# The mLSTM's two key groups as one pair of seven products, woven with a query group and the value groups

## The chip, the cores and the metric

The kernel runs on one core of one Trainium2 chip. The time is the device time of one execution in microseconds; of the kernel before, three runs gave 2150.21 to 2151.62 us, with a median of 2151.44 us.

## The reference

One layer of an encoder trunk over 256 rows of 2048 channels, in float32. Two SwiGLU feed-forward blocks stand around a mixer, each followed by a layer norm. The mixer multiplies the first norm's output by one wide matrix and cuts the product into columns:

```python
x = _layer_norm(ALPHA * x + 0.5 * _swiglu(x, ffn1_w1[i], ffn1_w3[i], ffn1_w2[i]), ln1_g[i], ln1_b[i])
mix = _hybrid_mixer(x, w_in[i], b_gates_m[i], conv_m[i], norm_m[i], w_up_m[i], w_up_sb[i], w_out[i])
...
proj = x @ w_in
mq, mk, mv, mo, mi, mf, sq, sk, sv, ga, gb = _split_cols(proj)
qk = jax.nn.silu(_causal_conv(jnp.concatenate([mq, mk], axis=-1), conv_w))
q_m, k_m = jnp.split(qk, 2, axis=-1)
```

`mq` and `mk` are the mLSTM's queries and keys (1024 columns each, four heads of 256), `mv` its values, `mo` its output gates, `mi` and `mf` its input and forget gates (four columns each); `sq`, `sk` and `sv` belong to the stick-breaking attention, `ga` and `gb` gate the two branches' sum. Queries and keys go through a short causal convolution along the rows and a SiLU.

## The kernel before, in words

**Units, splits, queues.** TensorE multiplies in pieces: each weight block of 256 rows by 512 columns (`raw`, 128 partitions x 1024 values) and each activation tile is held as a high and a low half (`split`, `actT`), and three matmuls, high by high, high by low and low by high, make one product (L1468 to L1470). A *unit* is one block against one half (128) of the rows: two steps of 128 weight rows with three matmuls each, six of 128x512. A block comes in by a DMA on the SP queue (`loads`, L1370), ScalarE writes its high half (L1393), VectorE the low half (L1397), and only then can the unit's second matmul start. Six split blocks are held at a time in the mixer, and raw blocks up to a limit that depends on the stage (`HELD`: 6 in the stage "mix", 10 in "woven", 12 in "wide"). Raw blocks, splits, activation tiles and larger intermediate results (`big`) share 51 pages of SBUF.

**Plain groups and pairs.** A plain group (`group`) is 512 columns of a weight over all 2048 rows: 8 blocks, each used by two units, one for each half of the rows, so 16 units. A pair (`seven`, `both7`) takes two such groups together by a scheme of seven products in place of eight for each quarter of the weight's rows: 28 units, each with a block of its own. Some of these blocks are sums of raw blocks. Each sum is either an addition on VectorE (L444) or, for the quarters listed in `loaded`, a DMA on GpSimd's queue that adds onto the raw block (L450). `every` lists all quarters, with two sums by VectorE in each; `later` leaves out the first, whose four sums are all VectorE's. A pair also needs a second kind of activation tiles, its *forms*, sums and differences of the halves of the transposed rows (`form_turn`, L382 to L386, then split by L358 and L359). The results of the seven products are put together by `both7`'s `done` and `rest` on ScalarE and VectorE.

**Order.** The program is a list of units, with small generators beside it that fall due at written delays (`sched.spawn`). Pairs stand in a `side` list that `weave` distributes among the plain units of a `main` list in proportion. Each engine works through its own instructions in the order in which the program made them.

**Around the change.** The first norm transposes its rows in pieces (`Norm.turn`, L363), applies gain and bias to the transposed values (L295) and splits them into the tiles of `x1T`. With `ActT(..., True)` the transposed values lie in a temporary tile that is dropped, and `forms_later` (L394 to L401) later adds the high and low halves again (L399) and makes the forms. The norm's rows themselves are scaled by VectorE (`affine`, L622), their bias is added by a DMA on GpSimd's queue (L626), and each then leaves for DRAM on the SP queue (`put_away`, L331). After the first feed-forward block come the first query group (16 units), the group with the gates and two stick-breaking heads (16 units of 264 columns), the second query group and the two key groups, all plain. Then two value groups, the stick-breaking columns and the branch gates follow as `main`, woven with five pairs as `side`. A query or key group is copied to two temporary tiles by `qk_done`, and `conv` transposes it, runs the convolution on VectorE (L890) and the SiLU on ScalarE. `gates` (L827 to L855) and the generators `mlstm`, `stick` and `gated` run beside the units, each as soon as its inputs are flagged.

Of the kernel before, what the change touches and what calls it, by code (L numbers as in the profile page):

```python
# [11 lines left out]
ALU = mybir.AluOpType  # L12
# [225 lines left out]
def kernel(  # L238
# [39 lines left out]
    def big(shape=(P, 1024)):  # L278
        return page_pool.tile(list(shape), F32, name="big", tag="page")
# [113 lines left out]

    def forms_later(act, c):  # L394

        act.whole[c] = big()
        for t in range(TT):
            hi, lo = (act.tiles[c, t][:, k].rearrange("q k s -> q (k s)") for k in range(2))
            nc.vector.tensor_tensor(out=act.whole[c][:, t * COL:(t + 1) * COL], in0=hi, in1=lo, op=ALU.add)  # L399
        yield 4.0  # L400
        yield from form_turn(act, c)  # L401


    def rows_of(w, r, col0, cols):
# [350 lines left out]

    x1T = ActT(act_tile, ActT(act_tile), True)
    norm1 = Norm(ln1_g[0], ln1_b[0], gb1, x1T, (24.0, 3.0), put_away)
# [101 lines left out]
    def qk_done(which, g):  # L859
        stage = {}  # L860

        def done(ps, t):
            stage[t] = temp()
            nc.scalar.copy(stage[t][:], ps)
            if t == TT - 1:
                sched.spawn(conv(which, g, stage), DELAY["cv0"])
        return done

    def conv(which, g, stage):
        for e in range(2):  # L870
# [25 lines left out]
            yield DELAY["cv2"]  # L896
        drop(2)

# [207 lines left out]
    program.extend(flat(group(w_in, range(0, D, 2 * P), 4096, 2 * HM + 2 * DS, x1T, gates_done)))  # L1106
    for which, g in ((0, 1), (1, 0), (1, 1)):
        program.extend(flat(group(w_in, range(0, D, 2 * P), which * 1024 + g * COL, COL, x1T, qk_done(which, g))))
        if which == 0:
            program.append(lambda: [sched.spawn(forms_later(x1T, c), 4.0 + 12.0 * c) for c in range(4)])  # L1110
    program.append(lambda: [sched.spawn(in_sequence([mlstm(a), mlstm(a + 1)])) for a in (0, 2)])

    def v(g):
# [70 lines left out]
    def pair(g):  # L1184
# [4 lines left out]
    gate = branch(0, 1)  # L1189
    main = v(0) + v(1) + sb(*SB_GROUPS[0]) + sb(*SB_GROUPS[1]) + [Mode("wide")] + sb(*SB_GROUPS[2]) + sb(*SB_GROUPS[3]) + [lambda: sched.spawn(lane())] + branch(0, 0) + gate[:4] + bring_ym_back(gate[4:] + ups(0)) + ups(1) + ups(2)  # L1190
    mode("woven")
    program.extend(weave(main, in_line([both7(w_in, sq0 + 2 * HS * DS, sq0 + 2 * HS * DS + COL, x1T, sv_dest, sv_ready, later),
                                   both7(w_in, 3072, 3072 + COL, x1T, mo_dest, mo_ready, every), pair(1), pair(2), pair(3)])))
    mode("mix")
# [164 lines left out]
    def pieces(j):  # L1359
        return [slice(0, 1), slice(1, 2)] if j < 2 else [slice(0, 2)]  # L1360

    def loads(most=len(raws)):
        while pos["load"] < most and pos["raw"] < (4 if pos["at"] < 6 else limits(pos["split"])[0]):
            j = pos["load"]
            r = raws[j]
            r.tile = page_pool.tile([P, 2, COL], F32, name="raw", tag="page")
            dst, src = r.tile[:, :, :r.cols], r.src
            if r.cols == COL:
                dst, src = whole(dst), whole(src)
            nc.sync.dma_start(out=dst, in_=src)  # L1370
            pos["load"] += 1
            pos["raw"] += 1

    def make(j):
# [9 lines left out]
    def split_one():  # L1384
# [15 lines left out]
        pos["split"] += 1  # L1400
        for f in w.soon:
            assert f.raw.tile is not None
            f.make()
            f.made = True
        pos["raw"] -= len(w.frees)
# [120 lines left out]
```

## Time and profile before

| | |
|---|---|
| median of three runs | 2151.44 us |
| the profiled execution | 2150.85 us |
| its span, first to last instruction | 2149.1 us |
| share of TensorE, weight loads, VectorE, ScalarE, GpSimd | 100%, 83%, 87%, 70%, 7% |
| granted TensorE clock | 1.00 |
| DMA traffic | 537 MB, 250 GB/s in the mean |

The span is cut into instructions with start, duration and the instruction or transfer that ended the wait before them. Engines are named PE (TensorE), PEld (its weight loads), DVE (VectorE), ACT (ScalarE), POOL (GpSimd) and SP (the queue of most DMAs). Records of neighbouring matmuls overlap, as do those of neighbouring VectorE instructions, so what one costs in a row is read from start to start. L numbers are lines of the kernel before, unless a row of the new order is shown. The mixer begins near 688 us.

### The profile page before, as it was taken

The numbers are of one execution on the slowest core, as the hardware profiler recorded it, in microseconds if no ns is written. First come the engines' busy times: TensorE is split into PE (matmuls) and PEld (weight loads), VectorE is DVE, ScalarE is ACT, GpSimd is POOL, SyncE is SP. The second block draws the span as 40 slices with busy tenths as digits, with TensorE's granted clock in tenths as the row PEclk, the third lists the DMA queues.
The fourth block names the chain that finished last, engine by engine and source line by source line (L and its number), as shares of the span: only waits on it lengthen the run. The fifth ranks groups of instructions, "written<-read, shape, count | busy, mean of one in ns | idle before, by whom it ended". The sixth has DMA issues, their size and how long they took to land. (4 is left out here: it accounts for less than half of the span.)

```text
span 2149.1 us, 27832 instructions
## 1 busy us (share of the span) xinstructions
PE 2140.6 (100%) x9742; PEld 1774.0 (83%) x9742; DVE 1864.1 (87%) x2002; ACT 1499.8 (70%) x1947; POOL 161.1 (7%) x190
## 2 busy tenths in 40 slices
PE   9999999999999999999999999999999999999998
PEld 7888888888888888888888888888888888888887
DVE  7899989899987798878888999799998998989763
ACT  6676777767767665778876667757676776776872
POOL 0011000011000000000000000011000011000000
PEclk9999999999999999999999999999999999999999
DMA  9799788988894776868898888789878898889562
GB/s 363 232 265 268 245 264 245 280 266 272 263 310 156 213 262 200 257 205 217 261 282 264 269 235 293 236 226 264 263 246 249 275 279 263 262 260 282 216 180 109
DMA packets 151963, 537.02 MB, mean 250 GB/s; under 512 B 17168, under 2 KB 21776, under 8 KB 151824
## 3 DMA queue, kind: packets, MB, share of 16 engines
q1 hardware_dynamic: 125616, 439.82, 57.2%
q0 software_dynamic: 26208, 95.43, 23.7%
q8 instruction: 76, 1.25, 0.2%
q14 instruction: 63, 0.52, 0.1%
HBM read 528.90 MB, written 6.29 MB: 249 GB/s over the span
## 5 line engine op out<-in xcount | busy, mean ns | idle before, releaser
L1397 DVE TENSOR_TENSOR split<-raw,split 128x1024 fp32r<-128x1024 f32 (+1 forms) x1102 | 1294.8, 1210 | 157.5 <-ACT split L1393 148.7
L1393 ACT CAST split<-raw 128x1024 fp32r<-128x1024 f32 (+1 forms) x1102 | 1106.9, 1043 | 353.6 <-DVE raw L444 118.4
L1468 PE MATMUL mm<-split,actT 128*128 128x512 f32 x3056 | 1196.8, 392 | 0.5 <-ACT actT L358 0.4
L1470 PE MATMUL mm<-split,actT 128*128 128x512 f32 x3056 | 1183.9, 387 | 0.0
L1469 PE MATMUL mm<-split,actT 128*128 128x512 f32 x3056 | 1182.9, 387 | 0.6 <-DVE split L1397 0.4
L1470 PEld LDWEIGHTS mm<-split,actT 128*128 128x128 f32 x3056 | 573.7, 188 | 118.8 <-DVE actT L359 0.4
L1469 PEld LDWEIGHTS mm<-split,actT 128*128 128x128 f32 x3056 | 574.4, 188 | 114.9 <-DVE split L1397 2.1
L1468 PEld LDWEIGHTS mm<-split,actT 128*128 128x128 f32 x3056 | 574.1, 188 | 114.8 <-issue 1.0
L444 DVE TENSOR_TENSOR raw<-raw 128x1024 f32<-128x1024 f32 x214 | 260.7, 1220 | 2.3
L450 POOL DMA_DIRECT2D raw<-in_ffn_w_dram x124 | 109.0, 998 | 1028.5 <-DVE split L1397 883.2
L359 DVE TENSOR_TENSOR actT<-temp,actT 128x512 fp32r<-128x512 f32 (+1 forms) x94 | 62.6, 682 | 49.3 <-ACT actT L358 49.3
L295 ACT ACTIVATE temp<-mm 128x512 f32<-128x512 f32 (+1 forms) x54 | 31.2, 583 | 76.4 <-PE mm L1470 76.2
L718 ACT COPY big<-mm 128x512 f32<-128x512 f32 x80 | 46.8, 585 | 28.9 <-PE mm L1470 28.5
L358 ACT CAST actT<-temp 128x512 fp32r<-128x512 f32 (+1 forms) x94 | 56.9, 616 | 13.0 <-DVE temp L383 7.1
L450 POOL DMA_DIRECT2D raw<-in_w_in_dram x38 | 33.3, 990 | 407.5 <-DVE split L1397 394.9
L371 ACT COPY temp<-ms 128x512 f32<-128x512 f32 x44 | 25.9, 588 | 44.4 <-PE ms L363 43.8
L725 ACT COPY mm<-big 128x512 f32<-128x512 f32 x96 | 55.8, 589 | 0.0
L662 DVE TENSOR_TENSOR temp<-mm,temp 128x512 f32<-128x512 f32 x72 | 49.6, 688 | 5.0 <-PE mm L1470 3.8
L626 POOL DMA_DIRECT2D big<-in_ln_b_dram x12 | 10.4, 865 | 351.7 <-DVE big L622 218.2
L1313 DVE TENSOR_TENSOR temp<-temp,big 128x512 f32<-128x512 f32 (+1 forms) x10 | 5.8, 584 | 32.5 <-ACT temp L295 32.5
L291 ACT ACT_TABLE_LOAD x26 | 33.4, 1283 | 0.5
L359 DVE TENSOR_TENSOR actT<-big,actT 128x512 fp32r<-128x512 f32 x24 | 16.4, 689 | 11.6 <-ACT actT L358 11.6
(140 smaller groups left out, 636.1 us busy)
## 6 DMA issues: line engine op xcount, KB each, us to landing
raw<-in_ffn_w_dram SPq DMA_DIRECT2D x528, 512.0 KB, 6.2
raw<-in_w_in_dram SPq DMA_DIRECT2D x168, 512.0 KB, 5.6
raw<-in_ffn_w_dram POOLq DMA_DIRECT2D x124, 512.0 KB, 8.8
raw<-in_w_in_dram POOLq DMA_DIRECT2D x38, 512.0 KB, 8.3
raw<-in_w_out_dram SPq DMA_DIRECT2D x32, 512.0 KB, 4.7
raw<-in_w_ple_gate_dram SPq DMA_DIRECT2D x32, 512.0 KB, 4.5
raw<-in_w_up_m_dram SPq DMA_DIRECT2D x16, 512.0 KB, 6.1
raw<-in_w_up_sb_dram SPq DMA_DIRECT2D x16, 512.0 KB, 4.7
```

The source lines that it names most:

```text
L358: nc.scalar.copy(hi, ps)
L359: nc.vector.tensor_tensor(out=lo, in0=ps, in1=hi, op=ALU.subtract)
L444: nc.vector.tensor_tensor(out=out.tile[:, :, :cols], in0=a.tile[:, :, :cols], in1=b.tile[:, :, :cols], op=ALU.add)
L450: nc.gpsimd.dma_start(out=whole(out.tile[:]), in_=whole(src), accum_op=ALU.add)
L662: nc.vector.tensor_tensor(out=out, in0=a, in1=b, op=op)
L718: nc.scalar.copy(xres(t, g * COL), ps)
L725: nc.scalar.copy(ps, xres(t, g * COL))
L1393: nc.scalar.copy(hi[:, ks], r[:, ks])
L1397: nc.vector.tensor_tensor(out=lo[:, ks], in0=r[:, ks], in1=hi[:, ks], op=ALU.subtract)
L1468: nc.tensor.matmul(ps, hi, w[0][:, k, :u.cols], start=first, stop=False, skip_group_check=u.onto)
L1469: nc.tensor.matmul(ps, hi, w[1][:, k, :u.cols], start=False, stop=False, skip_group_check=u.onto)
L1470: nc.tensor.matmul(ps, lo, w[0][:, k, :u.cols], start=False, stop=last, skip_group_check=u.onto)
```

## The change

The two key groups become one pair (`both7` with `later`), with `k_dest`, `k_ready` and a `conv` that leaves its stage tiles alone when they aren't temporary. The pair is woven with the second query group, of which four units go ahead, and with the two value groups; `main` then begins with the stick-breaking columns. `sv`'s pair, now the second, takes `every` instead of `later`. The first norm's transposed rows are kept in pages, and the forms are made from them right behind the norm, so `forms_later` goes. The stage "woven", with its 10 raw blocks, begins with the second query group. A sum that a transfer makes is put off until its raw block has been issued (`sums_due`).

```diff
-    def forms_later(act, c):
-
-        act.whole[c] = big()
-        for t in range(TT):
-            hi, lo = (act.tiles[c, t][:, k].rearrange("q k s -> q (k s)") for k in range(2))
-            nc.vector.tensor_tensor(out=act.whole[c][:, t * COL:(t + 1) * COL], in0=hi, in1=lo, op=ALU.add)
-        yield 4.0
-        yield from form_turn(act, c)
...
-    x1T = ActT(act_tile, ActT(act_tile), True)
+    x1T = ActT(act_tile, ActT(act_tile))
...
-                sched.spawn(conv(which, g, stage), DELAY["cv0"])
+                sched.spawn(conv(which, g, stage, True), DELAY["cv0"])
...
-    def conv(which, g, stage):
+    def k_dest(k, t):
+        if ("k", t) not in st:
+            st["k", t] = big()
+        return st["k", t][:, k * COL:(k + 1) * COL]
+
+    def k_ready(k, t):
+        flags.add(("k", k, t))
+        if ("k", k, 0) in flags and ("k", k, 1) in flags:
+            st["convs"] = st.get("convs", []) + [conv(1, k, [k_dest(k, h) for h in range(TT)], False)]
+            if len(st["convs"]) == 2:
+                sched.spawn(in_sequence(st["convs"]), DELAY["cv0"])
+
+    def conv(which, g, stage, temps):
...
-    for which, g in ((0, 1), (1, 0), (1, 1)):
-        program.extend(flat(group(w_in, range(0, D, 2 * P), which * 1024 + g * COL, COL, x1T, qk_done(which, g))))
-        if which == 0:
-            program.append(lambda: [sched.spawn(forms_later(x1T, c), 4.0 + 12.0 * c) for c in range(4)])
...
-    main = v(0) + v(1) + sb(*SB_GROUPS[0]) + sb(*SB_GROUPS[1]) + [Mode("wide")] + sb(*SB_GROUPS[2]) + sb(*SB_GROUPS[3]) + [lambda: sched.spawn(lane())] + branch(0, 0) + gate[:4] + bring_ym_back(gate[4:] + ups(0)) + ups(1) + ups(2)
+    main = sb(*SB_GROUPS[0]) + sb(*SB_GROUPS[1]) + [Mode("wide")] + sb(*SB_GROUPS[2]) + sb(*SB_GROUPS[3]) + [lambda: sched.spawn(lane())] + branch(0, 0) + gate[:4] + bring_ym_back(gate[4:] + ups(0)) + ups(1) + ups(2)
+    side = in_line([both7(w_in, 1024, 1024 + COL, x1T, k_dest, k_ready, later),
+                    both7(w_in, sq0 + 2 * HS * DS, sq0 + 2 * HS * DS + COL, x1T, sv_dest, sv_ready, every),
+                    both7(w_in, 3072, 3072 + COL, x1T, mo_dest, mo_ready, every), pair(1), pair(2), pair(3)])
+    first = flat(group(w_in, range(0, D, 2 * P), COL, COL, x1T, qk_done(0, 1))) + v(0) + v(1)
     mode("woven")
-    program.extend(weave(main, in_line([both7(w_in, sq0 + 2 * HS * DS, sq0 + 2 * HS * DS + COL, x1T, sv_dest, sv_ready, later),
-                                   both7(w_in, 3072, 3072 + COL, x1T, mo_dest, mo_ready, every), pair(1), pair(2), pair(3)])))
+    program.append(lambda: [sched.spawn(in_sequence([mlstm(a), mlstm(a + 1)])) for a in (0, 2)])
+    program.extend(first[:4] + weave(first[4:], side[:28]) + weave(main, side[28:]))
...
+    waiting = []
+
+    def sums_due():
+        for f in [f for f in waiting if f.raw.tile is not None]:
+            waiting.remove(f)
+            f.make()
+            f.made = True
...
-        for f in w.soon:
-            assert f.raw.tile is not None
-            f.make()
-            f.made = True
+        waiting.extend(w.soon)
+        sums_due()
```

Counted over the whole program, TensorE has 24 matmuls of 128x512 fewer (8976 to 8952). VectorE has 12 weight splits (1082 to 1094), 8 sums of raw blocks (214 to 222) and 5 instructions of `both7`'s more, and the 8 additions of L399 fewer; ScalarE has 12 splits and 8 table loads (27 to 35) more; GpSimd issues 8 DMAs more (38 to 46 for this weight), SP as many as before.

How the order moves is seen first on VectorE, behind the group with the gates. Line L1397 (L1407 in the new kernel) is the low half of a weight split, L622 (L612) the norm's scaling, L830 to L832 (L820 to L822) the first instructions of `gates`, L434 a sum of raw blocks and L382 to L386 the form of one piece of the norm's output. Before:

```order
L1397 TENSOR_TENSOR split<-raw,split 128x1024 x2
L622 TENSOR_TENSOR big<-big 128x512
L1397 TENSOR_TENSOR split<-raw,split 128x1024 x2
L830 MEMSET big 4x256
L831 TENSOR_SCALAR big<-ms,bi 4x256
L832 TENSOR_SCALAR big<-ms,bf 4x256
L1397 TENSOR_TENSOR split<-raw,split 128x1024
L622 TENSOR_TENSOR big<-big 128x512
L1397 TENSOR_TENSOR split<-raw,split 128x1024
```

The splits here are those of the second query group and the first key group, with one or three short instructions between them. In the changed kernel the rows just behind the same `gates` instructions on VectorE are these:

```order
L434 TENSOR_TENSOR raw<-raw 128x1024
L1407 TENSOR_TENSOR split<-raw,split 128x1024
L382 TENSOR_TENSOR temp<-big 128x256
L383 SCALAR_TENSOR_TENSOR temp<-temp,big 128x256
L385 TENSOR_TENSOR temp<-big 128x256
L386 TENSOR_TENSOR temp<-big,temp 128x256
L612 TENSOR_TENSOR big<-big 128x512
L434 TENSOR_TENSOR raw<-raw 128x1024
L1407 TENSOR_TENSOR split<-raw,split 128x1024
L612 TENSOR_TENSOR big<-big 128x512
L1407 TENSOR_TENSOR split<-raw,split 128x1024 x2
```

Sums of the key pair and a form have moved in between the splits.

The second place is GpSimd's queue at the same point of the program, where L616 (L626 before) adds the first norm's bias and L440 (L450) makes a pair's sum. Before:

```order
L767 AFFINE_SELECT big<-big 4x512
L626 DMA big<-in_ln_b_dram 128x1024 x4
L450 DMA raw<-in_w_in_dram 128x1024 x38
L450 DMA raw<-in_w_out_dram 128x1024 x8
L626 DMA big<-in_ln_b_dram 128x1024 x3
```

There the four additions of the norm's bias followed one another, ahead of every sum of the mixer. In the changed kernel the same queue has:

```order
L757 AFFINE_SELECT big<-big 4x512
L616 DMA big<-in_ln_b_dram 128x1024
L440 DMA raw<-in_w_in_dram 128x1024
L616 DMA big<-in_ln_b_dram 128x1024
L440 DMA raw<-in_w_in_dram 128x1024
L616 DMA big<-in_ln_b_dram 128x1024
L440 DMA raw<-in_w_in_dram 128x1024
L616 DMA big<-in_ln_b_dram 128x1024
L440 DMA raw<-in_w_in_dram 128x1024 x43
```

Three of the key pair's sums stand between the norm's additions now.

More of the change, by code (lines that the diff above doesn't have):

```diff
@@ L896, in conv @@
             yield DELAY["cv2"]
-        drop(2)
+        if temps:
+            drop(2)
     def v_done(g):
@@ L1106 @@
     program.extend(flat(group(w_in, range(0, D, 2 * P), 4096, 2 * HM + 2 * DS, x1T, gates_done)))
-    for which, g in ((0, 1), (1, 0), (1, 1)):
-        program.extend(flat(group(w_in, range(0, D, 2 * P), which * 1024 + g * COL, COL, x1T, qk_done(which, g))))
-        if which == 0:
-            program.append(lambda: [sched.spawn(forms_later(x1T, c), 4.0 + 12.0 * c) for c in range(4)])
-    program.append(lambda: [sched.spawn(in_sequence([mlstm(a), mlstm(a + 1)])) for a in (0, 2)])
     def v(g):
@@ L1400, in split_one @@
         pos["split"] += 1
-        for f in w.soon:
-            assert f.raw.tile is not None
-            f.make()
-            f.made = True
+        waiting.extend(w.soon)
+        sums_due()
         pos["raw"] -= len(w.frees)
```

## The prediction

> **What bounds the kernel now.** I read the page first, then a table of stretches over the mixer's first half, then who TensorE waited for there.
>
> ```profile
> span 2149.1 us, 27832 instructions
> PE 2140.6 (100%) x9742; PEld 1774.0 (83%) x9742; DVE 1864.1 (87%) x2002; ACT 1499.8 (70%) x1947; POOL 161.1 (7%) x190
> ```
>
> A busy PE of 100% alone proves little, since matmul records overlap. The stretches, with columns PE, PEld, DVE, ACT, POOL busy, then granted clock, DMA share and GB/s, say more:
>
> ```profile
> 725.00:750.90 25.90, 25.90 (x122) 21.24 (x121) 20.71 (x29) 15.22 (x25) 1.73 (x2) 1.00 0.79 223
> 751.00:831.00 80.00, 79.96 (x364) 65.69 (x363) 76.40 (x109) 51.23 (x67) 6.12 (x7) 1.00 0.80 248
> 831.00:1100.00 269.00, 269.00 (x1277) 224.05 (x1277) 218.01 (x288) 204.90 (x322) 19.32 (x22) 1.00 0.78 235
> 1100.00:1260.00 160.00, 159.89 (x722) 132.26 (x721) 138.96 (x143) 102.31 (x120) 10.53 (x12) 1.00 0.87 272
> 1260.00:1340.00 80.00, 80.00 (x358) 66.24 (x358) 77.18 (x92) 54.97 (x67) 5.27 (x6) 1.00 0.81 259
> ```
>
> The only wait of TensorE that the profile names between 687 and 1360 us:
>
> ```profile
> PE ms L363 <- DVE big L586: 0.7, 1, 0.7
> ```
>
> So TensorE is fed throughout: it bounds the kernel by the number of its matmuls. Behind it stands VectorE, which has two very full stretches, 751 to 831 (76.40 of 80) and 1260 to 1340 (77.18 of 80), and keeps up by the blocks it split in advance. The start of a seven-product pair falls in the first of them.
>
> TensorE's own rows give the price of a matmul (their starts, not their 0.39 us of duration), and the places that I need below:
>
> ```profile
> 724.97 0.39 PE L1468 MATMUL mm<-split,actT 128*128 128x512 f32 x1
> 725.19 0.39 PE L1469 MATMUL mm<-split,actT 128*128 128x512 f32 x1
> ...
> 742.32 0.39 PE L1468 MATMUL mm<-split,actT 128*128 128x512 f32 x1
> 742.54 0.39 PE L1469 MATMUL mm<-split,actT 128*128 128x512 f32 x1
> ...
> 750.94 0.39 PE L1468 MATMUL mm<-split,actT 128*128 128x512 f32 x1
> 751.17 0.39 PE L1469 MATMUL mm<-split,actT 128*128 128x512 f32 x1
> ...
> 813.68 0.39 PE L1468 MATMUL mm<-split,actT 128*128 128x512 f32 x1
> 814.11 0.50 PE L1469 MATMUL mm<-split,actT 128*128 128x512 f32 x1
> ```
>
> Starts lie 0.227 us apart, so a unit of six matmuls takes 1.36 us. 724.97 is the first 512-wide unit after the gates' group; 742.32 begins the 13th such unit and 750.94 the 19th (18 units are 24.5 us; the transposes among them make up the rest).
>
> **The matmuls removed.** Two plain groups are 32 units, a pair of seven products is 28. Four units of six matmuls go: 24 x 0.227 = 5.4 us, all on the path.
>
> **VectorE right behind the gates' group.** This term decides. The plain key groups needed one split for two units; the pair needs one for each, and sums too, and the change brings the second forms of the norm's output forward into the same stretch (the rows shown with the change: two sums and a form now stand between splits that followed each other with one short row between them). VectorE works in order, so a split waits for all of it, and the unit that uses the split waits for the split. Its prices, start to start, from rows of before where it never paused:
>
> ```profile
> 715.40 2.94 DVE L890 SCALAR_TENSOR_TENSOR temp<-ms,cw,temp 128x253 f32<-128x253 f32 x6 [0.89 <-ACT temp L295]
> 718.26 4.72 DVE L1397 TENSOR_TENSOR split<-raw,split 128x528 fp32r<-128x528 f32 x5
> 722.90 0.68 DVE L622 TENSOR_TENSOR big<-big 128x512 f32<-128x512 f32 x1
> ...
> 731.57 0.27 DVE L830 MEMSET big<- 4x256 f32 x1
> ...
> 732.67 1.23 DVE L1397 TENSOR_TENSOR split<-raw,split 128x1024 fp32r<-128x1024 f32 x1 [0.17 <-ACT split L1393]
> ...
> 739.35 0.41 DVE L838 SCALAR_TENSOR_TENSOR big<-big 4x256 f32<-4x256 f32 x1
> ...
> 742.00 1.21 DVE L1397 TENSOR_TENSOR split<-raw,split 128x1024 fp32r<-128x1024 f32 x1
> 743.14 0.67 DVE L622 TENSOR_TENSOR big<-big 128x512 f32<-128x512 f32 x1
> 743.74 1.21 DVE L1397 TENSOR_TENSOR split<-raw,split 128x1024 fp32r<-128x1024 f32 x1
> ...
> 788.03 0.42 DVE L382 TENSOR_TENSOR temp<-big 128x256 f32<-128x256 f32 x1
> ...
> 789.50 1.22 DVE L444 TENSOR_TENSOR raw<-raw 128x1024 f32<-128x1024 f32 x1
> 790.63 2.35 DVE L1397 TENSOR_TENSOR split<-raw,split 128x1024 fp32r<-128x1024 f32 x2
> 792.90 1.29 DVE L359 TENSOR_TENSOR actT<-temp,actT 128x512 fp32r<-128x512 f32 x2
> 794.11 1.22 DVE L1397 TENSOR_TENSOR split<-raw,split 128x1024 fp32r<-128x1024 f32 x1
> ...
> 817.50 9.17 DVE L1397 TENSOR_TENSOR split<-raw,split 128x1024 fp32r<-128x1024 f32 x8
> 826.70 1.23 DVE L444 TENSOR_TENSOR raw<-raw 128x1024 f32<-128x1024 f32 x1
> ```
>
> A full split is 9.20 / 8 = 1.15; a gates split 0.60 (4.64 for two of them and three full ones); a sum 1.13; a scaling 0.60; a form 1.47 and its two low halves 1.21; the six steps of a convolution 2.86 (715.40 to 718.26); the gates 1.10 and 2.65. The convolution at 715.40 is in both programs the first thing behind the gates' opening splits, and it waited for ScalarE, so it can't start sooner. From it, the new order has, up to and with the split that the 19th wide unit needs: 2 convolutions (5.7), 4 forms (5.9), 3 pairs of low halves (3.6), 2 gates splits (1.2), 13 full splits (15.0), 3 sums (3.4), 5 scalings (3.0), and the gates (3.8): 41.5 us. That split is done at 715.4 + 41.5 = 756.9. The unit's second matmul, the first to use a low half, ran at 751.17. TensorE stands still for **5.7 us** in sum. The largest single gap is at the 13th unit: up to its split the same rows add to 30.4 (745.8), against 742.54, so 3.3. Behind the 19th unit the forms are over and the sum falls back below TensorE's pace.
>
> The sum takes VectorE as never waiting; with a pause or two like those in the rows (0.17 to 0.89) it is 5.7 to 8. Below 5.2 it can hardly come, as the prices repeat.
>
> A rule of the Trainium skill speaks for more: VectorE: DVE Perf Modes, section The DRAIN you can't avoid, says that the next operation does not start until the pipe has emptied. The trace disagrees: eight splits take 9.20 us, though one's record is 1.22 long, so the next starts 0.07 earlier. By the rule, 29 independent instructions of the sum would each cost about 0.08 more, 2.3 us, and the time would be 2155.3.
>
> **What goes.** At 814.11 a matmul started 0.43 behind the last instead of 0.227: the small wait at the old place of the overload, 0.2 us. Eight additions go from there too:
>
> ```profile
> L399 DVE TENSOR_TENSOR big<-actT 128x512 f32<-128x512 f32 x8 | 5.1, 685 | 0.0
> ```
>
> TensorE waited 0.2 in that stretch, so their 5.1 us give it nothing more.
>
> **The queues.** SP holds four put-aways (L331) among its loads, each waiting for GpSimd's addition to land:
>
> ```profile
> SPq L331 <- DMA big<-in_ln_b_dram: 38.6, 4, 11.8
> ...
> 729.04 0.33 SPq L331 DMA_DIRECT2D away<-big  x1
> ...
> 744.05 0.33 SPq L331 DMA_DIRECT2D away<-big  x1
> ...
> raw<-in_w_in_dram POOLq DMA_DIRECT2D x38, 512.0 KB, 8.3
> ```
>
> In the new order GpSimd's queue has the pair's additions (L440) between the norm's (L616). The norm's second waits for a scaling at 715.4 + 30.4 + 0.6 = 746.4; the pair's addition behind it lands some 8.3 us after its issue, near 756, and its block is first used seven units behind the 19th, near 756.7 + 7 x 1.36 = 766. Nine us are spare: I take nothing, and a landing of over 17 us would be felt. The second put-away moves by the same delay, from 744.05 to some 752; the loads behind it feed blocks first used 15 units behind the 19th, near 777, so they have time too.
>
> **The rest of the mixer.** Five pairs, 140 side units, were woven with 168 wide main units from the value columns on; now with 136, from the stick-breaking columns on. The change adds eight table loads in all:
>
> ```profile
> L291 ACT ACT_TABLE_LOAD x26 | 33.4, 1283 | 0.5
> ```
>
> The loads are 8 x 1.28 = 10.3 us of ScalarE, which was busy 205 of 269 us and covers them. VectorE's weight work (a split for each side unit and for each two main units, 8 sums a pair, 10 in the one pair whose first quarter is summed without transfers) rises from (224 x 1.15 + 42 x 1.13) / (308 x 1.36) = 73% of TensorE's time to (208 x 1.15 + 40 x 1.13) / (276 x 1.36) = 76%. It was busy 218 of 269 and 139 of 160 us; on average that leaves room. Bursts may not fit: the nearest rows are the stretches at 96%, which cost TensorE 0 to 0.04 us, and at the other end the 5.7 above. I take 1.5, near the rows that carried such a load; nothing there can gain.
>
> **The sum.** The profiled execution took 2150.85 us (span 2149.1). 2150.85 - 5.4 - 0.2 + 5.7 + 1.5 = 2152.4. The median lies 0.6 above that execution, so **2153.0 us**. A measurement here tells about 0.2% from no change, 4.3 us: no change that can be told.
>
> **Rivals.** *The blocks in hand suffice.* Then only the removed matmuls show: 2151.44 - 5.4 - 0.2 = 2145.8. For it: TensorE met no wait in the whole mixer, even at 95% of VectorE. Against: that stretch was entered with blocks split well ahead, the new one follows the norm. It needs the 41.5 us of work to be done in some 36. Chance 0.13.
>
> *The denser second half starves TensorE, slower.* Place: the bursts behind 831 us where forms, stick-breaking steps and a pair's sums meet. It decides as soon as a burst exceeds VectorE's lead; the price is that of the first overload once more, 5.7 instead of 1.5: 2157.2. For it: the 96% at 1260 to 1340. Against: 81% and 87% in the stretches before. Chance 0.27.
>
> *The clock falls in the gap.* At the end, with TensorE idle, the granted clock does fall:
>
> ```profile
> 2144.00:2147.50 3.50, 0.00 (x0) 0.00 (x0) 1.56 (x4) 0.19 (x1) 0.00 (x0) 1.00 0.27 91
> 2148.00:2149.00 1.00, 0.00 (x0) 0.00 (x0) 0.00 (x0) 0.00 (x0) 0.00 (x0) 0.50 0.00 0
> ```
>
> The last matmul ends before 2144 (none is busy in either row), and the clock is full until 2147.5 and half from 2148: it fell about 4 us into the idle time. A gap of 3.3 us stays short of that. If it fell, some 4 us at half speed would lose 2: 2155.0. The Trainium skill (TensorE: Matmul & The Clock Gate, HAM oscillation) puts the limit at idle gaps over about 3.4 us, which the gap just misses; the trace's 4 agrees roughly. Chance 0.05.
>
> **Chances and range.** Forecast 0.55, the others as given. Faster 0.13, same 0.55 + 0.05 = 0.60, slower 0.27. The forecast alone spans 2151.0 (5.2 and 0) to 2155.3 (8 and 1.5). The range goes up to 2159.5, a first overload of 8 with one of 5.7 behind it, and down to 2148.5, half of the first one hidden (2151.44 - 5.6 + 2.85 = 2148.7); it leaves out the full gain and little else.
>
> **What would show it.** In the profile after, TensorE's waits should name the split's low half, L1407, with 5 to 8 us in sum between 735 and 765, the longest near 3; VectorE should be over 95% busy from 715 to 760 and easier at 790 to 830; 24 matmuls fewer. No such wait, or one that names a DMA or lies behind 831, would make the reasoning wrong.

## The result and the profile after

| | before | changed |
|---|---|---|
| median of five runs each | 2151.24 us (2150.21 to 2151.62) | 2169.21 us (2166.19 to 2171.27) |
| ratio, 95% interval | | 1.0083 (1.0071 to 1.0094) |
| profiled execution, span | 2150.85, 2149.1 us | 2170.70, 2168.7 us |

The changed kernel is 0.8% slower, 18.0 us in the medians. The forecast was 2153.0 with a range to 2159.5. The head of the page after, whose matmul count is 24 lower:

```profile
span 2168.7 us, 27905 instructions
...
PE 2143.6 (99%) x9718; PEld 1772.8 (82%) x9718; DVE 1885.1 (87%) x2019; ACT 1523.6 (70%) x1966; POOL 168.1 (8%) x198
```

The same stretches as before the change, with columns PE, PEld, DVE, ACT and POOL busy, granted clock, DMA share and GB/s, and then two that the prediction named:

```profile
725.00:750.90 25.90, 23.49 (x106) 18.40 (x105) 25.62 (x40) 17.35 (x27) 3.49 (x4) 1.00 0.67 180
751.00:831.00 80.00, 74.53 (x330) 60.11 (x329) 69.02 (x78) 45.98 (x55) 6.95 (x8) 1.00 0.88 253
831.00:1100.00 269.00, 260.11 (x1216) 214.32 (x1215) 219.70 (x296) 206.29 (x311) 19.32 (x22) 0.98 0.73 220
1100.00:1260.00 160.00, 159.42 (x711) 131.87 (x710) 142.40 (x151) 112.09 (x137) 14.04 (x16) 1.00 0.90 284
...
735.00:760.00 25.00, 20.30 (x87) 15.07 (x85) 24.79 (x38) 17.05 (x23) 3.92 (x5) 1.00 0.86 233
790.00:830.00 40.00, 40.00 (x178) 33.09 (x177) 35.58 (x34) 23.81 (x27) 1.75 (x2) 1.00 0.77 234
```

TensorE now stands still in three of the four, and behind 831 us its clock isn't whole. What it waited for between 687 and 1360 us (line waited for: us in total, times, longest):

```profile
PE mm L1477 <- DVE split L1407: 7.7, 4, 2.7
PE ms L997 <- DVE temp L892: 2.6, 1, 2.6
PE ms L1079 <- DVE actT L1075: 2.6, 1, 2.6
PE ms L982 <- DVE temp L892: 1.4, 1, 1.4
PE ms L792 <- ACT big L797: 1.3, 1, 1.3
PE mm L1476 <- ACT big L295: 0.9, 1, 0.9
PE ms L877 <- ACT temp L854: 0.5, 2, 0.3
PE mm L1476 <- ACT split L1403: 0.2, 1, 0.2
```

The first line is what the prediction spoke of. All others are waits of small products, the transposes and little matmuls of the mLSTM (L982, L997), of the stick-breaking steps (L792, L1079) and of the convolutions (L877), or of accumulators that wait to be read out, but for 0.2 us at a high half (L1476 behind L1403).

A fuller account comes from TensorE's own rows: from each matmul to the next, the time beyond the median for its line and shape, summed where it is over 0.06 us. It holds waits and half clock alike (us, profiled executions; the last three kernels are told below under these names; the changed kernel's execution lay 1.5 us over its median, and that of kplain was its slowest, 3.3 us over its median):

| stretch | before | changed | kplain | convcopy | combo8 |
|---|---|---|---|---|---|
| 700 to 800 | 1.2 | 10.8 | 1.2 | 8.6 | 1.9 |
| 800 to 950 | 3.4 | 10.9 | 3.5 | 4.0 | 5.6 |
| 950 to 1050 | 1.8 | 3.0 | 1.7 | 3.0 | 2.1 |
| 1050 to 1200 | 1.6 | 8.1 | 10.8 | 7.9 | 3.6 |
| sum | 7.9 | 32.7 | 17.1 | 23.5 | 13.2 |

From before to changed it grows by 24.8; less the 5.4 of the removed matmuls that is 19.4, and the spans differ by 19.6. So the account is closed, and the stretches say where to look: about 6 us at 743 to 766, 2.9 at 786, 7.5 around 860 to 877, 5.8 between 1050 and 1100.

The place at 859 to 871 us in rows. First TensorE, and then VectorE's convolutions of the keys (L892) and the mLSTM's scaling of scores (L984):

```profile
858.96 0.39 PE L1478 MATMUL mm<-split,actT 128*128 128x512 f32 x1
860.79 1.55 PE L982 MATMUL ms<-qk 128*128 128x256 f32 x8 [1.45 <-DVE temp L892]
...
867.88 0.40 PE L1478 MATMUL mm<-split,actT 128*128 128x512 f32 x1
870.89 1.20 PE L997 MATMUL ms<-big,temp 128*128 128x257 f32 x2 [2.61 <-DVE temp L892]
```

```profile
857.71 2.93 DVE L892 SCALAR_TENSOR_TENSOR temp<-ms,cw,temp 128x253 f32<-128x253 f32 x6
...
864.50 0.56 DVE L984 SCALAR_TENSOR_TENSOR temp<-ms,temp 128x384 f32<-128x384 f32 x1
...
867.80 2.94 DVE L892 SCALAR_TENSOR_TENSOR temp<-ms,cw,temp 128x253 f32<-128x253 f32 x6 [0.18 <-ACT temp L295]
```

Neither small matmul reads what L892 writes. L997's operand was ready with L984 at 865.06; it started 0.15 us after the end of a convolution at 870.74 that reads the PSUM tile `ms`. L982 started 0.15 after the one before it (860.64). A wait that names the reader of another `ms` tile points to a wait for its PSUM bank; `convcopy` below tests it. A seven-product pair holds five of the eight banks (m1 with m2, m7 with m4, m3, m5, m6), the main group two, so one is left for every small product; in the built program these two matmuls use the bank of the convolution ahead of them. The small products of the mLSTM and of the stick-breaking steps keep a written distance of 3 us on it (`bank`), the convolutions don't. In the kernel before, the keys' convolutions ran between 775 and 812 us, ahead of the mLSTM's first small matmul at 834.5 us.

### The profile page after: what moved, and what is told of

The parts are those of the page before. It is cut to its first block, busy times and chain, and to the rows that moved or that the text cites. A ratio compares the mean times of both kernels' runs of the same rounds, so it can differ in the third digit from the quotient of the medians.

```text
span 2168.7 us, 27905 instructions
## 1 busy us (share of the span) xinstructions
PE 2143.6 (99%) x9718; PEld 1772.8 (82%) x9718; DVE 1885.1 (87%) x2019; ACT 1523.6 (70%) x1966; POOL 168.1 (8%) x198
## 5 line engine op out<-in xcount | busy, mean ns | idle before, releaser
L1407 DVE TENSOR_TENSOR split<-raw,split 128x1024 fp32r<-128x1024 f32 (+1 forms) x1114 | 1308.3, 1211 | 151.9 <-ACT split L1403 142.5
L1403 ACT CAST split<-raw 128x1024 fp32r<-128x1024 f32 (+1 forms) x1114 | 1120.9, 1043 | 381.1 <-DVE raw L434 123.6
L1476 PE MATMUL mm<-split,actT 128*128 128x512 f32 x3048 | 1195.7, 392 | 1.2 <-ACT big L295 0.9
L1477 PE MATMUL mm<-split,actT 128*128 128x512 f32 x3048 | 1182.0, 388 | 8.3 <-DVE split L1407 8.2
L1477 PEld LDWEIGHTS mm<-split,actT 128*128 128x128 f32 x3048 | 573.8, 188 | 124.1 <-DVE split L1407 11.4
L1476 PEld LDWEIGHTS mm<-split,actT 128*128 128x128 f32 x3048 | 573.6, 188 | 115.9 <-ACT big L295 1.3
L434 DVE TENSOR_TENSOR raw<-raw 128x1024 f32<-128x1024 f32 x222 | 270.7, 1220 | 8.5 <-DMA raw<-in_w_in_dram 6.2
L440 POOL DMA_DIRECT2D raw<-in_ffn_w_dram x124 | 109.0, 1003 | 1028.6 <-DVE split L1407 934.4
L359 DVE TENSOR_TENSOR actT<-temp,actT 128x512 fp32r<-128x512 f32 (+1 forms) x86 | 57.1, 681 | 39.2 <-ACT actT L358 39.2
L440 POOL DMA_DIRECT2D raw<-in_w_in_dram x46 | 41.0, 1004 | 427.0 <-DVE split L1407 281.6
L358 ACT CAST actT<-temp 128x512 fp32r<-128x512 f32 (+1 forms) x86 | 52.1, 616 | 17.5 <-DVE temp L383 12.3
L359 DVE TENSOR_TENSOR actT<-big,actT 128x512 fp32r<-128x512 f32 x32 | 21.9, 689 | 22.2 <-ACT actT L358 22.2
L616 POOL DMA_DIRECT2D big<-in_ln_b_dram x12 | 10.3, 862 | 350.2 <-issue 191.3
```

Source lines behind the costliest of these rows:

```text
L358: nc.scalar.copy(hi, ps)
L359: nc.vector.tensor_tensor(out=lo, in0=ps, in1=hi, op=ALU.subtract)
L434: nc.vector.tensor_tensor(out=out.tile[:, :, :cols], in0=a.tile[:, :, :cols], in1=b.tile[:, :, :cols], op=ALU.add)
L440: nc.gpsimd.dma_start(out=whole(out.tile[:]), in_=whole(src), accum_op=ALU.add)
L1403: nc.scalar.copy(hi[:, ks], r[:, ks])
L1407: nc.vector.tensor_tensor(out=lo[:, ks], in0=r[:, ks], in1=hi[:, ks], op=ALU.subtract)
```

## Experiments

Times are medians; each was run beside the kernel before on its chip, which took 2150.9 to 2151.4 us. Lines are those of the changed kernel unless said otherwise.

### Four single cures

The K pair is woven 12 units later (`start16`):

```diff
-    program.extend(first[:4] + weave(first[4:], side[:28]) + weave(main, side[28:]))
+    program.extend(first[:16] + weave(first[16:], side[:28]) + weave(main, side[28:]))
```

> The changed kernel with one number changed: the weave of the K pair's units into the query and value groups begins after 16 of these units in place of 4, about 12 to 16 us later; every operation stays. Late-inputs theory (the time is lost at a few separate places, at each of which TensorE's queue stands at an operand that comes a little late, and each place is cured by more room there): the four waits at 743 to 756 us and the two small ones at 765 and 766, 6.0 us in sum, fall to under 1.5 us, and the time goes from 2169.2 to about 2164; the waits behind 850 us stay as they are. Load theory (VectorE has too much work for the stretch, wherever the units stand): the same work is packed closer behind 757 us, waits of 4 to 6 us turn up between 757 and 800 us, and the time stays at 2168 to 2171.

2164.4 us, 1.0060 (1.0043 to 1.0076). The four waits for low halves are gone. In their place the profile has, at 740 to 760 us, one long wait:

```profile
PE ms L877 <- ACT temp L854: 3.6, 1, 3.6
```

The second query group now ended earlier, and its transposes stood in TensorE's queue ahead of their staged copies, which stood on ScalarE behind a form that VectorE made late (3.83 us; the same chain as in `forms_early` below). Behind this wait the clock was half for 6.83 us, so by the account the profiled execution lost about as much at 735 to 780 us as without the edit, 6.8 against 7.3. What it gained lies at 786 us (3.0 less) and at 845 to 900 us (1.3 less). The edit removes the waits that it aimed at, but a fixed delay elsewhere no longer fits, and the profile doesn't show that the time gained is theirs.

More room ahead of the mLSTM's first heads (`mlstm20`):

```diff
-        yield bank(0.0)
+        yield 20.0 * (1 - h % 2); yield bank(0.0)
```

> The changed kernel with 20 us more written delay ahead of the first head of each of the two mLSTM lanes; every operation stays. Late-inputs theory: the mLSTM's small matmuls at 859 and 868 us no longer come to TensorE ahead of the VectorE work behind the keys' convolutions, so the gaps of 1.6, 2.8 and 0.9 us there go, and with them the half clock from 870 us (together 9 us of the starts beyond nominal between 850 and 900 us): about 2161. Load theory: VectorE's queue is behind for the whole stretch, the gap moves to the next small matmul or split, and the time stays within 2167 to 2171.

2167.6 us, 1.0076 (1.0061 to 1.0092): 1.6 less, not 8. The 9.2 us of the stretch 850 to 900 fell to 2.7, as the first theory had it, but the heads now met other small products. Three waits of its profile between 1077 and 1103 us, of which the first was there without the edit (2.6):

```profile
PE ms L1079 <- DVE actT L1075: 1.9, 1, 1.9
...
PE ms L1078 <- ACT big L295: 1.6, 1, 1.6
PE ms L1038 <- DVE big L1032: 1.5, 1, 1.5
```

Another head's first matmul (L972) waited 1.7 us at 874 us for a key convolution that it doesn't read. The load theory's answer, that the wait moves on, came true here, though not for VectorE's splits.

Later put-aways (`away16`):

```diff
-                    sched.spawn(self.away(t, k), DELAY["away"])
+                    sched.spawn(self.away(t, k), 16.0)
```

> The changed kernel with the first norm's put-aways issued 16 us of the written clock after their bias DMA in place of 5; every operation stays, only SyncE's order changes. If the load of the K pair's last block was held up on SyncE by the fourth put-away, which stood waiting for its bias DMA, the wait of 2.9 us at 786 us goes, and the time is about 2166. If VectorE's load sets that wait, it stays, and the time is within 1 us of 2169. If the put-aways' rows, held 11 us longer, now keep the loads waiting for pages, it is slower than 2170.

2165.7 us, 1.0067 (1.0052 to 1.0082), 3.5 less, and no wait at 786 us. But the next kernel's profile has none there either, though its program is that of the changed kernel up to about 970 us. That left the matter open (see cc_away).

More room for the triangle matmuls (`s1_9`):

```diff
-    "s1": 4.5,
+    "s1": 9.0,
```

> The changed kernel with the written delay ahead of the stick-breaking step's triangle matmuls 9 us in place of 4.5; every operation stays. Late-inputs theory: the wait of 2.7 us at 1091 us for the low half goes, and the half clock from 1095 us with it (6.7 us of starts beyond nominal between 1050 and 1100 us, 1.1 of it before another matmul): 2163.5 to 2165. Load theory: a wait of like size turns up at another of the steps, and the time stays at 2168 to 2171.

2163.5 us, 1.0056 (1.0041 to 1.0071), 5.8 less: the wait at 1091 us and its half clock are gone (6.7 us between 1050 and 1100 fell to 2.7, while 1100 to 1200 rose from 1.4 to 3.3). By the account of the profiled executions that is 2.1 us, of 6.4 between their spans. Most of the rest lies where both programs are still the same: 2.9 at 786 us and 1.4 at 845 to 900, where the half clock lasted 3.41 in place of 6.83 us. So the whole 5.8 is not shown to be this delay's.

### Order, bank or load

The keys as two plain (classical) groups in the pair's place (`kplain`):

```diff
-    side = in_line([both7(w_in, 1024, 1024 + COL, x1T, k_dest, k_ready, later),
+    side = [u for g in range(2) for u in flat(group(w_in, range(0, D, 2 * P), 1024 + g * COL, COL, x1T, qk_done(1, g)))]
+    side += in_line([
                     both7(w_in, sq0 + 2 * HS * DS, sq0 + 2 * HS * DS + COL, x1T, sv_dest, sv_ready, every),
...
-    program.extend(first[:4] + weave(first[4:], side[:28]) + weave(main, side[28:]))
+    program.extend(first[:4] + weave(first[4:], side[:32]) + weave(main, side[32:]))
```

> The changed kernel with the keys as two classical groups (32 units of 6 matmuls, 16 blocks) in the place of the K pair (28 units, 28 splits, 8 sums), woven the same way; forms, order and all else as in the changed kernel. It has 24 matmuls more (5.4 us). Bank theory (five accumulators of a seven-product pair and two of the main group leave one PSUM bank of eight for all small products, and the keys' convolutions, which are read by VectorE for some 3 us each and take no part in the written spacing of that bank, now meet the mLSTM there): the two groups hold two banks at a time, so the waits at 859 and 868 us and the half clock behind them go (9 us), the waits at 743 to 786 us go with the pair's splits (6 to 9 us), those behind 950 us stay: 2169.2 + 5.4 - 9 - 7.5 = 2158, between 2155 and 2161. Order theory (keys that come late bring the mLSTM too close to them, whatever the banks): the waits at 859 and 868 us stay in like size, and the time is 2165 to 2168.

2157.6 us, 1.0033 (1.0019 to 1.0046), where the bank theory had 2158. With 24 matmuls more it is 11.6 us faster than the changed kernel. Its waits from 687 to 1360 us (its lines behind the edit are one higher, L1408 for L1407):

```profile
PE mm L1478 <- DVE split L1408: 3.3, 2, 2.8
PE ms L1079 <- DVE actT L1075: 2.6, 1, 2.6
PE mm L1477 <- ACT big L295: 0.9, 1, 0.9
```

None lies ahead of 1072 us. So the pair, not the later place of the keys alone, makes the waits up to 870 us; the one at the triangle matmul belongs to the new order, since it stays without the pair.

The keys' convolutions spaced on the spare bank (`convbank`):

```diff
-            h = 2 * g + e
-            ps = misc([P, 2, S])
+            h = 2 * g + e; yield from () if temps else (sched.slot(0.0, 6.0),)
+            temps or bank(3.0); ps = misc([P, 2, S])
```

> The changed kernel with the keys' convolutions taking a slot of 6 us in the written spacing of the spare PSUM bank, which all other small products keep at 3 us; every operation stays. Bank theory: the score matmul that waited 1.6 us at 859 us no longer gets its bank right behind a convolution, and the next one at 868 us waits less, so 2 to 4.4 us go, and the half clock from 870 us (some 4 us) goes with the longer gap: 2161 to 2167. Load theory (VectorE's or ScalarE's work delays inputs, not banks): the waits stay in sum, 2168 to 2171.

2171.6 us, 1.0095 (1.0080 to 1.0110): a miss, 2.4 slower. The waits at 859 and 868 went; the spacing pushed everything behind them into new ones:

```profile
PE ms L792 <- ACT big L797: 2.4, 2, 2.2
PE ms L792 <- ACT temp L295: 2.3, 1, 2.3
```

Both are for the bank again: what ended them are ScalarE's readings of other `ms` tiles. Here the spacing only moved the waits, and added to them.

The forms alone, in the kernel before (`forms_early`):

```diff
-    x1T = ActT(act_tile, ActT(act_tile), True)
+    x1T = ActT(act_tile, ActT(act_tile))
...
-            program.append(lambda: [sched.spawn(forms_later(x1T, c), 4.0 + 12.0 * c) for c in range(4)])
+            pass
```

> The kernel before with one part of the change alone: the first norm keeps its transposed rows whole and makes the sum forms from them at the norm, without the eight additions later; the keys, their place and the weave stay as before. If the burst of VectorE at the gates' group needs the K pair's splits as well as the forms, the blocks in hand cover the forms, and the time stays within 1.5 us of before. If the forms alone overload VectorE there, waits for the low halves appear at 735 to 757 us, and it is 3 to 6 us slower than before. No wait of the mLSTM at 859 to 870 us and no half clock by any theory, unless the change's cost in the mixer comes from the forms.

2156.8 us, 1.0025 (1.0015 to 1.0035), 5.8 slower, the size that the prediction gave forms and pair together, but by another chain. ScalarE's rows in this kernel (L358 is a form's hi half, L864 the staged copy of the second query group), and the stretch behind it:

```profile
749.48 1.29 ACT L358 CAST actT<-temp 128x512 fp32r<-128x512 f32 x2 [3.83 <-DVE temp L383]
750.68 1.04 ACT L1393 CAST split<-raw 128x1024 fp32r<-128x1024 f32 x1
751.62 1.06 ACT L864 COPY temp<-mm 128x512 f32<-128x512 f32 x2
```

```profile
753.20:756.50 3.30, 3.30 (x9) 2.58 (x9) 3.30 (x5) 3.28 (x6) 0.00 (x0) 0.50 0.81 231
```

ScalarE's queue stood 3.83 us at a form for which VectorE was late; the copies stood behind it, TensorE's transposes behind those (3.15 and 0.38 us), and then the clock was half for 3.4 us.

Five cures together (`combo`): the later weave, the later put-aways, the longer `s1`, the slots of `convbank`, and

```diff
-                sched.spawn(conv(which, g, stage, True), DELAY["cv0"])
+                sched.spawn(conv(which, g, stage, True), DELAY["cv0"] + 5.0 * g)
```

> The changed kernel with five edits together: the weave of the K pair begins 12 units later, the put-aways are issued 16 us after their bias DMA, the triangle matmuls have 9 us of room, the keys' convolutions take a slot of 6 us of the spare bank, and the second query group's convolution starts 5 us later (for the wait of 3.8 us at 749 us that the later weave alone brought). Late-inputs and bank theories: the savings add, 2169.2 - 4.9 - 3.8 - 5.8 - 4, with the load wait at 786 us counted once: about 2150, between 2147 and 2155, so level with before or a little faster. Load theory: VectorE and ScalarE are full and each cure moves its wait on, 2158 to 2164.

2161.0 us, 1.0050 (1.0033 to 1.0066). It missed by 11: the two waits that the slots bring (2.4 and 2.4 us at 888 and 947) stayed, each with 3.41 us of half clock, which by the account is some 8 of the 11 (2.4 + 2.4 and 1.7 for each half clock).

### The bank by itself

The keys' columns leave PSUM by one copy before the convolution reads them (`convcopy`):

```diff
-            for k in range(2):
-                activate(acc[:, k], ps[:, k], ACT.Copy, scale=w(3, k))
+            c = ps if temps else temp().rearrange("q (k s) -> q k s", s=S); temps or nc.scalar.copy(c[:], ps[:]); ps = c
+            for k in range(2): activate(acc[:, k], ps[:, k], ACT.Copy, scale=w(3, k))
...
-            drop()
+            drop(1 if temps else 2)
```

> The changed kernel with the keys' transposed columns copied out of PSUM by one ScalarE instruction (128x512, four times in all) before the convolution reads them; VectorE's work stays and stands where it stood, ScalarE has some 2.5 us more. Bank theory: the bank is free after the copy in place of after VectorE's six steps, so the waits of 1.6 us at 859 and 2.8 us at 868 us that ended with VectorE's convolution, and the half clock from 870 us, go, with nothing pushed back behind them: 8 to 9 us less, about 2161. Load theory (the small matmuls wait since VectorE is late with their operands): the waits stay, 2168 to 2172.

2161.4 us, 1.0047 (1.0032 to 1.0062), 7.8 less than the changed kernel, with more work. TensorE and VectorE in this kernel:

```profile
857.10 1.47 PE L982 MATMUL ms<-qk 128*128 128x256 f32 x8
...
864.93 0.59 PE L997 MATMUL ms<-big,temp 128*128 128x257 f32 x2
```

```profile
855.63 2.95 DVE L892 SCALAR_TENSOR_TENSOR temp<-temp,cw 128x253 f32<-128x253 f32 x6
...
865.18 2.95 DVE L892 SCALAR_TENSOR_TENSOR temp<-temp,cw 128x253 f32<-128x253 f32 x6
```

The convolutions stand where they stood in the order and take as long (2.95 us). L982 now runs in the middle of the first, and L997 starts 0.25 us ahead of the second and ends inside it; neither waits. By the account 800 to 950 us fell by 6.9. VectorE's lateness is excluded here, and the bank is shown.

The combination with the copies in place of the slots, the query convolution 3 us later (`combo2`):

> The changed kernel with the K pair's weave 12 units later, the put-aways 16 us after their bias DMA, 9 us of room for the triangle matmuls, the second query group's convolution 3 us later, and the keys' columns copied out of PSUM (in place of the slot of 6 us for the bank). Bank theory: in the combination with slots 5 us of waits for the bank had moved to 888 and 947 us; here they don't arise, and the time is 2161 - 5 - 2 (half clocks) = about 2154, between 2150 and 2157. Load theory: another wait takes their place, 2158 to 2163.

2154.4 us, 1.0018 (1.0008 to 1.0027), as expected. Its full clock lasts to the end of TensorE's work.

The same with `"sbt": 8.0` in place of 4.6 (`combo3`):

> As the combination before it, with 8 us in place of 4.6 ahead of the stick-breaking heads' transposes, whose wait of 1.5 us at 964 us in the changed kernel ended with a ScalarE copy. Late-inputs theory: 1 to 2 us less than without this edit. Bank theory: that wait is for the bank that the former transposes hold until ScalarE has copied it, so a common delay moves both and gains nothing, or brings new meetings: within 3 us of the combination without it.

2161.5 us, 1.0048 (1.0033 to 1.0063): outside what either theory gave. The wait it aimed at stayed (1.48 us), and new ones of 0.8 to 1.8 came at 1046, 1073, 1121 and 1130 us. One delay moved by 3.4 us costs 7, which shows how closely the others are set around it.

The early forms with a later query convolution, in the kernel before (`forms_q1`, `DELAY["cv0"] + (4.0 if (which, g) == (0, 1) else 0.0)`):

> The kernel before with the forms made early, and the second query group's convolution 4 us later. If the whole 5.8 us of the early forms is the chain seen there (ScalarE's queue stood 3.8 us at a form's split that waited for VectorE, with the group's copies behind it, and TensorE's transposes behind those, then half a clock), it goes: 2151 to 2152.5. If the forms overload VectorE whatever waits for them, the wait moves to a low half between 745 and 760 us, and the time stays at 2155 to 2157.

2150.7 us, 0.9998 (0.9988 to 1.0007). The whole 5.8 us of the early forms was that chain. The eight additions that they save are worth nothing that shows.

### What is left

The weave 6 units later still (`first[:22]`), and the second query group's columns copied too, its convolution 4 us later (`combo5`, against `combo2`):

> As the combination with copied columns (2154.4), with the K pair's weave 6 units later still (18 in all), and the second query group's transposed columns copied out of PSUM too, its convolution 4 us later. If the 4.2 us of starts beyond nominal left at 752 to 776 us are the pair's first blocks and that convolution's bank, they go: 2150 to 2151, level with before. If the pair is now too dense ahead of the end of the value groups, low halves come late at 775 to 830 us instead: 2153 to 2156.

2154.1 us, 1.0015 (1.0006 to 1.0024). The two small gaps became one of 2.2 us at 765, with half a clock: no gain.

Without the later put-aways (`combo6`):

> The combination above without the later put-aways. If the put-aways hold up loads that the pair needs, it is 2 to 3.5 us slower than with them, with a wait for a low half between 775 and 800 us whose block's load came late; if the later weave already gives the loads room, the two are within 1 us.

2153.7 us, 1.0012 (1.0003 to 1.0021): the same.

The copies and the later put-aways alone (`cc_away`):

> The changed kernel with copied columns (2161.4) and the put-aways 16 us after their bias DMA. If the put-aways' queue costs its wait at 786 us in the median execution, and part of the one at 752 us, as the run with the later put-aways alone suggested: 2157.5 to 2159. If that wait comes in some executions only, by where the transfers fall: within 1 us of 2161.4.

2161.1 us, 1.0043 (1.0031 to 1.0056), against 2161.4 without the later put-aways: no difference.

Against `combo6`, the query convolution another 4 us later (`combo8`, `DELAY["cv0"] + 8.0 * g`):

> As the combination without later put-aways (2153.7), with the second query group's convolution 4 us later still. If its 2.9 us in VectorE's queue made the split at 763 us late, the gap of 2.1 us and the half clock behind it (3.6 us in sum) go: 2150 to 2151, level with before. If the sums and splits of the pair alone make it late, 1 to 2 us stay there: 2152 to 2153.5.

2150.6 us, 1.0001 (0.9992 to 1.0009). The gap and the half clock went. Its waits from 687 to 1360 us:

```profile
PE ms L792 <- ACT big L797: 1.3, 1, 1.3
PE mm L1477 <- DVE split L1407: 1.1, 2, 0.8
PE ms L363 <- DVE big L576: 0.8, 1, 0.8
PE ms L877 <- DVE temp L984: 0.3, 1, 0.3
PE ms L1090 <- ACT big L295: 0.3, 1, 0.3
PE ms L1090 <- DVE temp L942: 0.2, 1, 0.2
```

And with the forms spread (`combo9`, `18.0 + (8.0 if self.away else 5.0) * c`):

> As the run above, with the four forms of the first norm 8 us apart in place of 5, so that the last is made 9 us later. If the forms' burst still delays the blocks ahead of the pair's first units, this takes 1 to 2 us more away: 2149 to 2150, at or a little under before. If the pair's units now wait for the later forms, or the forms meet the first sums, it is 1 to 4 us slower than the run above.

2150.9 us, 1.0001 (0.9992 to 1.0010): no difference. So all 18 us come back with the four edits of `combo8` (the later weave, the longer `s1`, the copies, the later query convolution), which leave the change in place, but no version was faster than before: `combo8` has 13.2 - 7.9 = 5.3 us more beyond the nominal starts than before, just the 5.4 that its fewer matmuls save. These are small things, most of them at 900 to 1110 us. The largest, 1.5 us at 949, is the wait of the transposes that `combo3` aimed at and didn't cure; whether freeing that bank sooner cures it wasn't tried.

## Why the prediction was wrong

*The matmuls removed*, 5.4 us: right. The page counts 24 fewer, and the account closes with this number.

*VectorE right behind the gates' group*, 5.7 us: right in place, cause and sum. The waits of L1477 lie at 743.1 and 752.5 us (2.46 and 2.39, with two of 0.2 to 0.4), 5.5 us in sum; the largest was 2.5, not 3.3. VectorE was 24.79 of 25 us busy at 735 to 760 and 35.58 of 40 at 790 to 830. `kplain`, which keeps the forms and drops the pair's splits and sums, has no such wait; `start16` takes them away by room alone, though another wait then cost as much there.

*What goes*, 0.2 us: right. At 800 to 845 us the rows of the changed kernel hold nothing over nominal, before 0.7.

*The queues*, "I take nothing": failed for the profiled execution. I followed the second put-away and not the fourth:

```profile
SPq L331 <- DMA big<-in_ln_b_dram: 43.2, 4, 12.6
...
775.62 0.33 SPq L331 DMA_DIRECT2D away<-big  x1
776.04 13.72 SPq L1379 DMA_DIRECT2D raw<-in_w_in_dram  x8
...
787.04 1.23 DVE L434 TENSOR_TENSOR raw<-raw 128x1024 f32<-128x1024 f32 x1 [6.17 <-DMA raw<-in_w_in_dram]
...
789.46 0.50 PE L1477 MATMUL mm<-split,actT 128*128 128x512 f32 x1 [2.71 <-DVE split L1407]
```

The loads stood behind the put-away until 776.04, a sum waited 6.17 us for its block, and TensorE 2.71. In five profiles with these put-aways and this weave the gap beyond nominal was 2.9, 2.3, 1.2, 0.7 and 0; in the two with later ones there was none. The medians disagree (3.5 less in one pair of kernels, 0.3 in the other), so its price in the median is not settled.

*The rest of the mixer*, "I take 1.5": this is the step that failed. The account has 15.2 us there (24.8 less 9.6 ahead of 800), and waits behind 831 us are what the prediction itself named as a sign against it. I priced VectorE's weight work against TensorE's time, 76% of it, and that did leave room: the splits of that stretch cost 0.7 us. What I didn't count were the things that a pair holds while it runs. Moving a pair ahead of the keys' convolutions put them under a pair's five accumulators, one bank was left, and TensorE's queue stood at small matmuls for it: with the half clock 6.9 us of the account and 7.8 of the medians, shown by `convcopy`. The Trainium skill (Perfetto Trace Analysis, section Matmuls) says that groups should rotate through PSUM banks so that one is read out while the next runs; the traces agree, the 4.4 us of waits at 859 and 868 being what it costs when none is free. The other large part, 5.8 us at 1050 to 1100, is for the most part a written delay of 4.5 us that no longer fits the new order: `s1_9` removes the wait, and `kplain` keeps it without the pair. What the longer delay gains in the end lies between the 2.1 us of the profiles and the 5.8 of the medians. ScalarE had finished the high half at 1091.0, but VectorE got to the low one (L1075) late:

```profile
1091.12 0.68 DVE L504 SCALAR_TENSOR_TENSOR big<-mm,big 128x512 f32<-128x512 f32 x1
1091.72 0.69 DVE L506 TENSOR_TENSOR mm<-mm,big 128x512 f32<-128x512 f32 x1
1092.31 1.22 DVE L1407 TENSOR_TENSOR split<-raw,split 128x1024 fp32r<-128x1024 f32 x1
1093.45 0.55 DVE L1075 TENSOR_TENSOR actT<-temp,actT 128x384 fp32r<-128x384 f32 x1
```

That is the burst of the second rival, which had the right sign and the right stretch for this part; but it priced the whole stretch at 5.7, and its cause is the order of a few rows, not a denser second half: VectorE was busy 41.05 of 50 us at 1050 to 1100, and 43.03 before.

*The clock falls in the gap*, 0.05: it did, in the profiled execution at two other gaps (ahead of 870 and 1095 us), and at the first gap in the profiles of four other kernels with this order. The condition, that a gap of 3.3 us stays short, was wrong, as the last section shows. *The blocks in hand suffice*: excluded by the waits at 743 and 752.

## What to carry to other kernels

When a long-lived accumulation is moved, count what it holds as well as what it computes: the PSUM banks left for the small products that will run under it, and each product that takes part in no spacing rule. A wait that ends with an instruction whose output the waiting matmul doesn't read points to a buffer; in this kernel freeing the buffer sooner cured it and spacing didn't. Delays written for one order have to be checked again for every small step behind the place that changed.

## What was unexpected of the hardware

The granted clock fell at gaps of 2.1 to 3.2 us, and at one of 3.8. In the profiled execution of the changed kernel (columns as in the other stretches):

```profile
868.40:870.20 1.80, 0.00 (x0) 0.00 (x0) 1.73 (x4) 0.30 (x1) 0.00 (x0) 1.00 0.50 123
870.30:877.00 6.70, 6.11 (x14) 4.79 (x15) 4.43 (x5) 2.43 (x4) 1.71 (x2) 0.50 0.10 39
877.10:884.00 6.90, 6.90 (x33) 5.27 (x32) 3.21 (x7) 5.50 (x10) 0.00 (x0) 1.00 1.00 224
```

A gap of 2.8 us was followed by 6.83 us of half clock, which the gaps of 2.4 to 2.9 at 743, 752 and 786 us of the same execution were not. Over the profiles of all these kernels there are 34 gaps of 2.0 to 3.8 us beyond the nominal start in the mixer; behind 21 of them the clock fell, behind 13 not, with lengths mixed (2.1 fell, 2.9 did not). Below 2.0 none did (the longest of these was 1.9). Each fall lasted 3.41 or 6.83 us, and some began only after TensorE had gone on, by up to 1.5 us (the gap before 1094.05, the fall at 1095.51). The Trainium skill (TensorE: Matmul & The Clock Gate, sections What's actually happening and HAM oscillation) gives a free-running window of 3413 ns, with which the lengths agree, and gaps over about 3.4 us as what to avoid, which these runs contradict: 2.1 us were enough.

A fall costs little where VectorE is the one behind: in the four profiles whose clock fell at 745 us, the second gap at 752 us was 0.8 to 1.0 in place of 2.4, so the sum there stayed at about 6 us. Where TensorE is the bound, it costs its half: behind eleven other falls of 3.41 us the account has 1.6 to 2.1 us.
